# Two projection blocks beside the first layer's attention, and tiles of normalised tokens taken over by output weights chunk by chunk

## The chip, the core and the metric

The kernel runs on one core of a Trainium2 chip, with its engines TensorE (PE; its weight loads are PEld), VectorE (DVE), ScalarE (ACT), GpSimd (POOL) and SyncE (SP), which here only issues DMAs. The metric is the device time of one execution in microseconds. Before the change three timed runs took 2635.68, 2638.16 and 2638.88 us, median 2638.16 us.

## What is computed

One step of a small diffusion backbone with two layers, over 1024 sample tokens and 256 prompt tokens of 1024 features. The change is in layer 0, whose reference is, cut to what matters:

```python
hp = _rmsnorm(yp, norm_g[l]) * (1.0 + sc_p) + sh_p        # normalised tokens, samples alike
qa, ka, va, za, qb, kb, vb, ob, zb, gb = jnp.split(h @ w_in, AB_SPLITS, axis=-1)
attn = _window_attn_latent(_axial_rope(qa, rows, cols), _axial_rope(ka, rows, cols), va, ck, cv, sink)
a_out = attn * jax.nn.silu(za)                            # 16 heads, 4 key/value groups
hb, states = _mlstm_bidir(qb, kb, vb, ob, gb + gate_bias, conv_w, norm_w, init)
b_out = hb * jax.nn.silu(zb)
out = jnp.concatenate([a_out, b_out], axis=-1) @ w_out
yp = yp + gt_p * out_p
```

Layer 1 is a latent attention with its own projections. All products are made in float32r: each operand is split into a high and a low part, and three matmuls (high x high, high x low, low x high) take the place of one.

## The kernel before, in words

The normalised tokens lie transposed in SBUF as `hTh` and `hTl` (high and low), in three chunks of 512, 512 and 256 tokens, each one tile of 8 slices of 128 features. The input projection `h @ w_in` is cut into **blocks** of 256 output columns (`DenseBlock`). A block of attention queries (q) or of its gate (z) has six **units** (`unit_T`), two per chunk; a unit is 24 matmuls into one PSUM bank, of 512 or, for the last chunk, 256 columns. Its cost is 2 or 1, so a block costs 10. `Dense.units` gives the blocks out in pieces, in the order of the list `blocks`, and `Dense.pump` requests and splits the weights of the next block ahead of time.

Layer 0 goes through these stages. First the tokens are normalised and five blocks run with the adaLN rows beside them; here a scheduler of the framework orders the instructions. Then the order is written by hand (`manual_schedule`):

- `beside_memory`: 80 visits of the mLSTM in 174 slots (7 ahead, 2 for each visit, 7 behind), with 24 projection blocks (cost 240) spread evenly over the slots.
- `beside_attention`: the windowed attention of 4 groups x 10 query blocks. `Attention.run` goes through **ticks**. Each tick from 12 to 179 turns one block of 128 keys: PE transposes the probabilities (`turn`), ACT casts them (`split`, L1139) and DVE subtracts (L1140), and a tick later PE multiplies with the values (`weighted`) into one PSUM bank V that ACT and DVE empty at the group's end (`out`). Scores (`scores`), maximum (`peak`, DVE), exponential (`exp`, ACT) and division (`normal`, POOL) run some ticks ahead. `extra(i)` puts other work into tick i: until tick 12 the last block (z3), from tick 25 on **steps** of the output projection, 10 of them up to tick 56 and 150 evenly after that. A step is three matmuls of 512 columns; there are 200 steps over ten matrix rows, of which 160 run beside the attention.
- At tick 17 `release` gives back the token tiles (`hp`), the rope table (`rpool`) and the projection pools, opens the pool `wo1` in their place, and `load_wout` loads ten rows of 512 KB of `w_out`, one every three ticks, and splits each four ticks later in two halves (ACT L824, POOL L825).

The remaining 40 steps, the second half of the output projection and layer 1 follow. A helper issues every matmul (`Kern.mm`, L103), every transpose (L107) and every DMA (L138), so the profile tells these apart by tile names: `mm` is the bank of projections and transposed probabilities, `D` of scores, `V` of weighted values, `att_kh`/`att_q` keys and queries, `w` output weights, `o_ah`/`o_al` the split rows they multiply, `wh`/`wl` input weights.

## Time and profile before

| | |
|---|---|
| median of three timed runs | 2638.16 us |
| the profiled execution's own time | 2633.0 us |
| its span, first to last instruction | 2630.9 us |
| PE, DVE, ACT, POOL busy | 98%, 68%, 54%, 44% of the span |
| DMA | 348.78 MB, mean 133 GB/s |

Busy time is the union of an engine's instructions. Matmuls overlap, so PE can be busy all the time and still have room; the distance between starts tells more. Idle time is given to the engine whose signal ended it.

### The profile page before, as it was taken

The numbers are of one execution on the slowest core, as the hardware profiler recorded it, in microseconds if no ns is written. First come the engines' busy times: TensorE is split into PE (matmuls) and PEld (weight loads), VectorE is DVE, ScalarE is ACT, GpSimd is POOL, SyncE is SP. The second block draws the span as 40 slices with busy tenths as digits, with TensorE's granted clock in tenths as the row PEclk, the third lists the DMA queues.
The fourth block names the chain that finished last, engine by engine and source line by source line (L and its number), as shares of the span: only waits on it lengthen the run. The fifth ranks groups of instructions, "written<-read, shape, count | busy, mean of one in ns | idle before, by whom it ended". The sixth has DMA issues, their size and how long they took to land.

```text
span 2630.9 us, 48195 instructions
## 1 busy us (share of the span) xinstructions
PE 2573.1 (98%) x16209; PEld 2261.5 (86%) x16209; DVE 1782.9 (68%) x4040; ACT 1407.8 (54%) x3598; POOL 1164.6 (44%) x1533
## 2 busy tenths in 40 slices
PE   8999999999999999989999999999999999999998
PEld 6878898898998888878888878987799899999887
DVE  6884565746747566488777554335788888888853
ACT  5232444434533433287666432322788888888842
POOL 5342333423434444275554553223455545555742
PEclk9999999999999999999999999999999999999999
DMA  7465566556656655463433454233310101100333
GB/s 249 153 178 177 160 194 190 175 176 193 205 180 221 199 175 177 144 199 107 133 114 103 154 169 167 84 101 118 95 31 29 48 25 40 36 19 29 123 105 128
DMA packets 344584, 348.78 MB, mean 133 GB/s; under 512 B 29609, under 2 KB 291414, under 8 KB 344082
## 3 DMA queue, kind: packets, MB, share of 16 engines
q1 hardware_dynamic: 344338, 345.71, 42.6%
q8 instruction: 129, 2.11, 0.3%
q14 instruction: 117, 0.96, 0.1%
HBM read 235.09 MB, written 110.51 MB: 131 GB/s over the span
## 4 chain that ended last, share of the span: by engine, by line
PE 82%; DVE 5%; issue 2%; ACT 2%; DMA 2%; POOL 2%; SPq 0%; DVEq 0%; POOLq 0%; ACTq 0%
PE mm L103 34%; PE S L103 28%; PE V L103 8%; PE T L107 6%; PE D L103 3%; PE mm L107 2%; PE T L103 1%; DMA w<-in_w_out_ab 0%; DVE macc L321 0%; DVE att_nm L1114 0%; POOL wl L354 0%; ACT att_p L1119 0%; DMA kh<-scr 0%; DMA mw<-in_w_mod 0%; DVE cmx L2157 0%
## 5 line engine op out<-in xcount | busy, mean ns | idle before, releaser
L354 POOL TENSOR_TENSOR wl<-wf,wh 128x256 fp32r<-128x256 f32 (+2 forms) x288 | 244.4, 875 | 444.0 <-ACT wh L353 416.0
L103 PE MATMUL mm<-hTh,wh 128*128 128x512 f32 (+1 forms) x912 | 328.4, 360 | 0.9 <-DVE scr L620 0.9
L103 PE MATMUL mm<-hTl,wh 128*128 128x512 f32 (+1 forms) x912 | 325.1, 356 | 0.0
L103 PE MATMUL mm<-hTh,wl 128*128 128x512 f32 (+1 forms) x912 | 325.0, 356 | 0.0
L103 PE MATMUL S<-cK,cQ 96*128 96x512 f32 (+3 forms) x1248 | 297.9, 363 | 2.1 <-ACT cPb L2159 1.0
L2207 DVE TENSOR_TENSOR cpl<-T,cph 128x512 fp32r<-128x512 f32 x336 | 228.2, 684 | 37.4 <-ACT cph L2206 33.3
L103 PEld LDWEIGHTS S<-cK,cQ 96*128 96x128 f32 (+1 forms) x1248 | 192.7, 189 | 24.1 <-ACT cPb L2159 2.9
L2206 ACT CAST cph<-T 128x512 fp32r<-128x512 f32 x336 | 192.5, 589 | 26.1 <-PE T L107 13.6
L103 PEld LDWEIGHTS mm<-hTh,wl 128*128 128x128 f32 x912 | 171.7, 188 | 26.6
L103 PEld LDWEIGHTS mm<-hTh,wh 128*128 128x128 f32 x912 | 171.5, 188 | 25.1 <-DVE scr L620 1.1
L103 PEld LDWEIGHTS mm<-hTl,wh 128*128 128x128 f32 x912 | 171.7, 188 | 23.1
L2157 DVE TENSOR_REDUCE cmx<-S 128x1 f32<-128x512 f32 x256 | 172.4, 681 | 15.6 <-PE S L103 14.5
L103 PE MATMUL V<-cph,cV 128*128 128x256 f32 x672 | 176.8, 289 | 0.2 <-DVE cst L2131 0.2
L103 PE MATMUL V<-cpl,cV 128*128 128x256 f32 x672 | 171.9, 284 | 1.3 <-DVE cst L2131 1.3
L2138 POOL TENSOR_SCALAR cPa<-cPa,cst 128x512 f32<-128x512 f32 x128 | 99.7, 779 | 120.6 <-DVE cst L2135 94.3
L103 PE MATMUL S<-w,o_ah 128*128 128x512 f32 x492 | 151.5, 394 | 0.6 <-POOL w L825 0.6
L103 PE MATMUL mm<-w,o_ah 128*128 128x512 f32 x468 | 151.2, 402 | 0.0
L1128 POOL TENSOR_SCALAR att_p<-att_p,att_den 128x640 f32<-128x640 f32 (+1 forms) x128 | 97.7, 777 | 103.3 <-DVE att_den L1125 42.1
L1139 ACT CAST att_ph<-mm 128x512 fp32r<-128x512 f32 x168 | 98.6, 587 | 80.8 <-PE mm L107 78.6
L1140 DVE TENSOR_TENSOR att_pl<-mm,att_ph 128x512 fp32r<-128x512 f32 x168 | 115.7, 689 | 31.7 <-ACT att_ph L1139 26.7
L353 ACT CAST wh<-wf 128x256 fp32r<-128x256 f32 (+2 forms) x288 | 102.2, 410 | 64.3 <-DMA wf<-in_w_in_ab 34.3
L103 PE MATMUL mm<-wh,hTh 128*128 128x256 f32 x480 | 135.6, 283 | 0.0
(432 smaller groups left out, 7832.8 us busy)
## 6 DMA issues: line engine op xcount, KB each, us to landing
wf<-in_w_in_ab SPq DMA_DIRECT2D x120, 256.0 KB
in<-in SPq DMA_DIRECT2D x40, 514.0 KB
in<-in SPq DMA_DIRECT2D x32, 386.0 KB
mw<-in_w_mod SPq DMA_DIRECT2D x48, 256.0 KB
in<-scr SPq DMA_DIRECT2D x40, 258.0 KB
o_x<-y SPq DMA_DIRECT2D x20, 512.0 KB
wm<-in_w_mod SPq DMA_DIRECT2D x16, 512.0 KB
in<-cx SPq DMA_DIRECT2D x32, 256.0 KB
```

Source lines behind the costliest of these rows:

```text
L103: return self.nc.tensor.matmul(out, lhsT, rhs, start=start, stop=stop)
L107: self.nc.tensor.transpose(out, in_, self.ident[:p, :p])
L353: K.nc.scalar.copy(wh, wf[:, k])
L354: K.nc.gpsimd.tensor_sub(wl, wf[:, k], wh.bitcast(F32))
L1128: nc.gpsimd.tensor_scalar(pv, pv, den[:, i:i + 1], 1.0, ALU.mult, ALU.mult)
L1139: K.nc.scalar.copy(ph, self.T)
L1140: K.nc.vector.tensor_sub(pl, self.T, ph.bitcast(F32))
L2138: nc.gpsimd.tensor_scalar(pv, pv, wt[:, c:c + 1], rd, ALU.mult, ALU.mult)
L2157: nc.vector.tensor_reduce(mx[:, b, c:c + 1], S, AX.X, ALU.max, negate=True)
L2206: nc.scalar.copy(ph, T_)
L2207: nc.vector.tensor_sub(pl, T_, ph.bitcast(F32))
```

## The change

The list of blocks becomes q0, z0, q1, z1, q2, q3, z2, z3; before it alternated to the end. 23 blocks run beside the memory stage and two, z2 and z3, beside the attention: z2 until tick 12, z3 from tick 13 to tick 52 in pieces of three matmuls (six of the short chunk), one a tick (`parts = 4`). The output projection's steps begin at tick 61, 160 of them evenly to the attention's end.

The token tiles are cut smaller (`Hidden`): 20 tiles of one shape under one tag `hw`, two (in the last chunk four) slices of features in each. `place_wout` allocates 20 more under the same tag, so each row of output weights takes over the place of tokens whose last reader is z3. It loads halves of 256 KB into four raw buffers `wraw` and splits each three ticks later (six for the last four). The requests stand at ticks 30 to 44, every second, for the place of chunk 0; at 46 to 53, every one, for chunk 1; at 56 to 59 for chunk 2. `release` moves to tick 55 and no longer gives back the tokens' pool.

```diff
@@ -335,6 +335,7 @@
     def __init__(self, K, wp, cols, fn, bufs, width, src="w_in_ab"):
         self.K, self.wp, self.cols, self.fn, self.bufs, self.width = K, wp, cols, fn, bufs, width
         self.src, self.w, self.wf, self.when, self.asked = K.I[src][0], [], [], [], 0
+        self.parts = 2
 
     def ask(self):
         K, F, a = self.K, sum(n for _, n in self.cols), 2 * self.asked
@@ -371,10 +372,24 @@
                     yield u.cost / 2
             units = units[2:]
         for u in units:
-            n = u.cost if self.K.pairs else 2 * u.cost
+            n = u.cost * (1 if self.K.pairs else self.parts)
             for i in range(n):
                 u.products(i, n)
                 yield u.cost / n
+
+
+class Hidden:
+
+
+    def __init__(self, K, pool, N, tiles=None, cols=slice(None)):
+        self.shape, self.cols, self.m = [128, KD, N], cols, D // N
+        self.tiles = tiles or [K.t(pool, [128, self.m, N], F32R, "hw", 20) for _ in range(KD // self.m)]
+
+    def __getitem__(self, key):
+        _, k, s = key
+        if isinstance(k, slice):
+            return Hidden(None, None, self.shape[2], self.tiles, s)
+        return self.tiles[k // self.m][:, k % self.m, self.cols if s == slice(None) else s]
 
 
 class Unit:
@@ -662,11 +677,9 @@
     d["sd"] = [dram([NT, 128, 256], F32R, f"sd{h}") for h in range(4)]
     d["g"] = dram([4, NT, 2, 3, 128], F32, "grow")
 
-    K.hTh, K.hTl = [], []
     hp = right("hT0")
-    for ci, (t0, N) in enumerate(CHUNKS):
-        K.hTh.append(hp.tile([128, KD, N], F32R, tag=f"hh{ci}", name=f"hTh{ci}"))
-        K.hTl.append(hp.tile([128, KD, N], F32R, tag=f"hl{ci}", name=f"hTl{ci}"))
+    hidden = [[Hidden(K, hp, N) for _ in range(2)] for _, N in CHUNKS]
+    K.hTh, K.hTl = [[h[i] for h in hidden] for i in range(2)]
     wp = K.wp = right("w0")
     sp = left("start")
     setup_cond(K, sp)
@@ -730,8 +743,9 @@
     for h in range(4):
         blocks += b_proj(K, wp, tp, h)
     blocks.append(DenseBlock(K, wp, [(O_KA, 256)], partial(a_keys, K), 6, 272))
-    for g in range(4):
-        blocks += a_proj(K, wp, g)
+    qs, zs = zip(*[a_proj(K, wp, g) for g in range(4)])
+    blocks += [qs[0], zs[0], qs[1], zs[1], qs[2], qs[3], zs[2], zs[3]]
+    zs[3].parts = 4
     mp = left("mod")
     dense.mods = mod_steps(K, mp, mods[0:2], 4)
     K.tp = gtp = left("gtmp")
@@ -753,34 +767,43 @@
     K.y1 = [K.t(K.dram, [128, D], F32, f"y1_{t}") for t in range(NT)]
     K.y2 = [K.t(K.dram, [128, D], F32, f"y2_{t}") for t in range(NT)]
     w = I["w_out_ab"][0]
-    opened = []
+    opened = [hp]
+
+    wt = []
 
     def release():
-        for pool in (K.rpool, tp, wp, hp):
+        for pool in (stage, tp, wp):
             pool.release()
         K.ring = None
         p = right("wo1")
         opened.append(p)
-        wt = load_wout(K, p, w, [8, 9, 10, 11, 12, 13, 14, 15, 0, 1])
-        gate = gate_rows(K, p, 0)
+        gate = {}
+
+        def late():
+            gate[0], gate[1] = gate_rows(K, p, 0)
+
+        K.later(late, 8)
         steps = out_steps(K, p, Attention.ORDER, wt, lambda tt: gate[0 if tt < 8 else 1], lambda tt: x_src(K, tt),
                           lambda tt: ((d["bT"][tt], 0, 5), (d["bT"][tt], 5, 8, d["aT"][tt], 0, 2)), lambda tt: K.y1[tt])
         next(steps)
-        return steps
+        return steps, place_wout(K, hp, w, wt, p, [0, 1], 6)
 
     K.set_psum(S=3, mm=3, T=2)
     bp = left("mls")
     K.flow = Flow()
     with K.tc.manual_schedule():
         K.pairs = True
-        beside_memory(K, bp, dense, 24, 240)
+        beside_memory(K, bp, dense, 23, 230)
         K.pairs, K.spread = False, True
         bp.release()
         gp.release()
         K.set_psum(D=2, mm=3, V=1)
         ap = left("att")
         a_sinks(K, ap)
-        steps = beside_attention(K, ap, dense, release)
+        K.rpool.release()
+        stage = right("raw")
+        steps = beside_attention(K, ap, dense, place_wout(K, hp, w, wt, stage, [8, 9, 10, 11, 12, 13, 14, 15], 3),
+                                 release)
     K.flow = None
     ap.release()
     K.set_psum(S=5, T=3)
@@ -788,7 +811,8 @@
     wt = load_wout(K, p, w, range(2, 8))
     for _ in steps:
         pass
-    opened.pop().release()
+    while opened:
+        opened.pop().release()
     hp = K.hp1 = right("hT1")
     K.hTh, K.hTl = [], []
     for ci, (t0, N) in enumerate(CHUNKS):
@@ -811,6 +835,25 @@
             xst = []
     sp.release()
     p.release()
+
+
+def place_wout(K, p, src, wt, stage, ks, lag):
+
+
+    def split(w, wf):
+        wh, wl = w
+        K.nc.scalar.copy(wh, wf)
+        K.nc.gpsimd.tensor_sub(wl, wf, wh.bitcast(F32))
+
+    for k in ks:
+        w = [K.t(p, [128, D], F32R, "hw", 20) for _ in range(2)]
+        wt.append(w)
+        for half in range(2):
+            sl = slice(half * 512, half * 512 + 512)
+            wf = K.t(stage, [128, 512], F32, "wraw", 4)
+            K.dma(wf, src[k * 128:(k + 1) * 128, sl])
+            K.later(partial(split, [t[:, sl] for t in w], wf), lag)
+            yield
 
 
 def load_wout(K, p, src, ks):
@@ -1164,21 +1207,24 @@
         K.later(gated)
 
 
-def beside_attention(K, ap, dense, release):
+def beside_attention(K, ap, dense, place, release):
 
 
     A = Attention(K, ap)
-    units, spent, steps, left = dense.units(1), 0, None, 160
+    units, spent, steps, left = dense.units(2), 0, None, 160
     lead = A.LEAD + 1
-    n = lead + 4
+    n = lead + 42
+    asks = [*range(lead + 17, lead + 33, 2), *range(lead + 33, lead + 41), *range(lead + 43, lead + 47)]
 
     def extra(i):
-        nonlocal spent, steps, left
-        while spent < 10 and spent < max(3, (i + 1) * 10 / lead):
-            spent += next(units, 10)
+        nonlocal spent, steps, left, place
+        while spent < 20 and spent < max(3, (i + 1) * 10 / lead if i < lead else 10 + (i + 1 - lead) / 4):
+            spent += next(units, 20)
         if i == n:
-            steps = release()
-        while i > n + 8 and left > (160 - (i - n - 8) / 3 if i < n + 39 else 150 * (A.end - i) / (A.end - n - 39)):
+            steps, place = release()
+        if i in asks:
+            next(place)
+        while i > n + 5 and left > 160 * (A.end - i) / (A.end - n - 5):
             next(steps)
             left -= 1
 
@@ -1229,11 +1275,11 @@
         if n:
             K.later(lambda: (load_res(i + 1), K.dma(dst(t["tt"]), t["y"])))
 
-    load_res(0)
     load(0, 0)
-    K.later(partial(split, 0, 0), 5)
-    K.later(partial(load, 0, 1), 12)
-    K.later(partial(split, 0, 1), 17)
+    load(0, 1)
+    K.later(partial(split, 0, 0), 3)
+    K.later(partial(split, 0, 1), 5)
+    K.later(partial(load_res, 0), 7)
     yield
     for i in range(len(T)):
         ps = [None, None]
```

Three places in the order of instructions. On PE, at a tick near 13 (`small` is the identity of the transposes), before the change:

```order
L107 MATMUL mm_14361<-small,att_p_14100 128x128 x2
L107 MATMUL mm_14361<-small,att_p_14145 128x128 x2
L103 MATMUL V_14318<-att_ph_14344,att_v 128x512
L103 MATMUL V_14318<-att_pl_14345,att_v 128x512
L103 MATMUL D_14373<-att_kh,att_q_14189 128x384
L103 MATMUL D_14373<-att_kl,att_q_14189 128x384
L103 LDWEIGHTS mbf
L103 MATMUL D_14373<-mbf 128x128
L103 LDWEIGHTS mbf
L103 MATMUL D_14373<-mbf 128x128
L103 MATMUL D_14373<-att_kh,att_q_14189 128x256
L103 MATMUL D_14373<-att_kl,att_q_14189 128x256
```

and now, where `hw` are token tiles and `wh`, `wl` the weights of z3:

```order
L107 MATMUL mm_14132<-small,att_p_13928 128x128 x2
L107 MATMUL mm_14132<-small,att_p_13973 128x128 x2
L103 MATMUL mm_14162<-hw_129,wh_13870 128x512
L103 MATMUL mm_14162<-hw_133,wh_13870 128x512
L103 MATMUL mm_14162<-hw_129,wl_13871 128x512
L103 MATMUL V_14166<-att_ph_14103,att_v 128x512
L103 MATMUL V_14166<-att_pl_14104,att_v 128x512
L103 MATMUL D_14169<-att_kh,att_q_14017 128x384
L103 MATMUL D_14169<-att_kl,att_q_14017 128x384
L103 LDWEIGHTS mbf
L103 MATMUL D_14169<-mbf 128x128
L103 LDWEIGHTS mbf
```

Between the transposes and the next product with the values stand three matmuls of z3, one piece; before, that place held nothing in most of these ticks.

On POOL, around ticks 49 to 56 now (`L846` is the subtraction for the output weights, before at L825):

```order
L846 TENSOR_TENSOR hw_15259<-wraw_15260,hw_15258 128x512
L1204 TENSOR_TENSOR att_o_15323<-att_o_15323,att_z_15148 128x256
L1171 TENSOR_SCALAR att_p_15307<-att_p_15307,att_den_15309 128x512 x2
L846 TENSOR_TENSOR hw_15259<-wraw_15294,hw_15258 128x512
L846 TENSOR_TENSOR hw_15339<-wraw_15340,hw_15338 128x512
L1171 TENSOR_SCALAR att_p_15387<-att_p_15387,att_den_15389 128x640 x2
L846 TENSOR_TENSOR hw_15339<-wraw_15369,hw_15338 128x512
L846 TENSOR_TENSOR hw_15414<-wraw_15415,hw_15413 128x512
L1204 TENSOR_TENSOR att_o_15473<-att_o_15473,att_z_15302 128x256
L1171 TENSOR_SCALAR att_p_15457<-att_p_15457,att_den_15459 128x640 x2
L846 TENSOR_TENSOR hw_15414<-wraw_15443,hw_15413 128x512
L1171 TENSOR_SCALAR att_p_15533<-att_p_15533,att_den_15535 128x640 x2
```

and before, around ticks 37 to 43, where the same subtractions stood:

```order
L1128 TENSOR_SCALAR att_p_14893<-att_p_14893,att_den_14895 128x640 x2
L1220 TENSOR_TENSOR o_al_14938<-o_a_14784,o_ah_14937 128x384
L825 TENSOR_TENSOR w_14942<-w_14438,w_14941 128x512
L1128 TENSOR_SCALAR att_pp_14958<-att_pp_14958,att_den_14960 128x256 x2
L825 TENSOR_TENSOR w_15028<-w_14439,w_15027 128x512 x2
L1128 TENSOR_SCALAR att_pp_15010<-att_pp_15010,att_den_15012 128x256 x2
L1161 TENSOR_TENSOR att_o_15051<-att_o_15051,att_z_14923 128x256
L825 TENSOR_TENSOR w_15120<-w_14440,w_15119 128x512
L1128 TENSOR_SCALAR att_p_15077<-att_p_15077,att_den_15079 128x640 x2
L825 TENSOR_TENSOR w_15120<-w_14440,w_15119 128x512
L1128 TENSOR_SCALAR att_p_15136<-att_p_15136,att_den_15138 128x640 x2
L825 TENSOR_TENSOR w_15200<-w_14441,w_15199 128x512
```

The subtractions have moved to later ticks and stand as closely between the divisions `att_p`, one tick's worth each.

On ACT, near the end of the start stage, the casts of tokens into their high part, before (`hTh_129`, `131`, `133` are the three chunks):

```order
L537 CAST hTh_133<-xT_169 128x256 x3
L262 ACTIVATE mrow_433<-S_416 2x256
L537 CAST hTh_133<-xT_169 128x256
L537 CAST hTh_129<-xT_167 128x512
L537 CAST hTh_131<-xT_168 128x512
L537 CAST hTh_133<-xT_169 128x256
L262 ACTIVATE mrow_485<-S_468 2x256
L537 CAST hTh_129<-xT_167 128x512
L537 CAST hTh_131<-xT_168 128x512
L537 CAST hTh_133<-xT_169 128x256
```

and now (`hw_129` to `132` are chunk 0, `137` to `140` chunk 1, `145` and `146` chunk 2):

```order
L552 CAST hw_131<-xT_181 128x512
L262 ACTIVATE mrow_595<-S_578 2x256
L552 CAST hw_132<-xT_181 128x512
L552 CAST hw_137<-xT_182 128x512 x2
L552 CAST hw_138<-xT_182 128x512 x2
L552 CAST hw_132<-xT_181 128x512
L552 CAST hw_139<-xT_182 128x512 x2
L552 CAST hw_140<-xT_182 128x512 x2
L552 CAST hw_145<-xT_183 128x256 x4
L552 CAST hw_146<-xT_183 128x256 x4
```

Chunks 1 and 2 were cast as their slices came; now they all stand behind the last tile of chunk 0.

## Rows read from the trace of the kernel before

**Rows 1.** The page: PE's busy time, and the granted clock in 40 slices, in tenths.

```profile
PE 2573.1 (98%) x16209; PEld 2261.5 (86%) x16209; DVE 1782.9 (68%) x4040; ACT 1407.8 (54%) x3598; POOL 1164.6 (44%) x1533
...
PEclk9999999999999999999999999999999999999999
```

**Rows 2.** The table of stretches: from and to in us from the span's start, the length, then busy us (instructions) of PE, PEld, DVE, ACT and POOL, granted clock, DMA share and GB/s.

```profile
260.00:1084.00 824.00, 821.76 (x5338) 744.05 (x5337) 501.92 (x1281) 341.64 (x914) 319.83 (x391) 1.00 0.60 184
1084.00:1109.00 25.00, 25.00 (x147) 21.35 (x146) 8.44 (x21) 6.46 (x15) 3.37 (x5) 1.00 0.55 169
1109.00:1191.00 82.00, 74.04 (x470) 59.01 (x469) 68.58 (x156) 69.59 (x161) 61.00 (x72) 1.00 0.63 187
1191.00:1209.00 18.00, 16.90 (x108) 13.76 (x107) 14.80 (x32) 12.57 (x28) 8.49 (x11) 1.00 0.27 76
1209.00:1484.00 275.00, 275.00 (x1678) 233.45 (x1677) 211.44 (x460) 185.22 (x422) 140.79 (x182) 1.00 0.38 112
1484.00:1600.00 116.00, 114.74 (x521) 93.37 (x520) 50.42 (x78) 36.06 (x69) 59.24 (x52) 1.00 0.60 195
```

**Rows 3.** The timeline of PE at the end of the memory stage and in the lead: start, duration, and the matmul; between the first two rows stand 30 like them, between the last two 11.

```profile
1083.81 0.39 PE L103 MATMUL mm<-hTl,wh 128*128 128x512 f32 x1
...
1091.00 0.39 PE L103 MATMUL mm<-hTh,wl 128*128 128x512 f32 x1
1091.23 0.28 PE L103 MATMUL D<-att_kh,att_q 128*128 128x256 f32 x1
...
1102.74 0.28 PE L103 MATMUL mm<-hTh,wh 128*128 128x256 f32 x1
...
1104.16 0.34 PE L103 MATMUL D<-att_kh,att_q 128*128 128x384 f32 x1
```

**Rows 4.** The cast that each tick makes once, in the stretches 1109 to 1191, 1191 to 1209 and 1209 to 1484 us: count, duration in ns, first and last start. The first stretch ends with the cast that opens the next.

```profile
L1139 ACT CAST att_ph<-mm x41: 576/587/607, 1109.1 to 1190.6; 128x512 fp32r<-128x512 f32 x41
...
L1139 ACT CAST att_ph<-mm x8: 573/586/588, 1190.6 to 1206.9; 128x512 fp32r<-128x512 f32 x8
...
L1139 ACT CAST att_ph<-mm x120: 584/587/597, 1209.0 to 1483.5; 128x512 fp32r<-128x512 f32 x120
```

**Rows 5.** Groups of PE by shape: the matmuls of the output projection from 1109 to 1191 us (first two) and from 1209 to 1484 us: count, busy us, mean ns.

```profile
L103 PE MATMUL mm<-w,o_ah 128*128 128x512 f32 x18 | 5.8, 404 | 0.0
L103 PE MATMUL mm<-w,o_al 128*128 128x512 f32 x9 | 3.6, 395 | 0.0
...
L103 PE MATMUL mm<-w,o_ah 128*128 128x512 f32 x289 | 92.8, 402 | 0.0
L103 PE MATMUL mm<-w,o_al 128*128 128x512 f32 x144 | 57.0, 396 | 0.0
```

**Rows 6.** The view of waits of PE (1085 to 1195 us) and of ACT (1109 to 1195 us), the longest of each: us in total, times, longest.

```profile
PE V L103 <- DVE att_o L1158: 5.2, 8, 1.3
...
ACT att_p L1119 <- DVE att_nm L1114: 5.9, 10, 0.9
ACT att_ph L1139 <- PE mm L107: 4.2, 8, 1.1
ACT att_p L1119 <- POOL att_pp L1128: 1.0, 1, 1.0
```

**Rows 7.** The view of waits of PE in the memory stage, 260 to 1110 us, its longest.

```profile
PE mm L103 <- DVE scr L620: 0.9, 1, 0.9
```

**Rows 8.** Durations: the gate's multiplication and tanh of a z unit (min/median/max ns, 1084 to 1120 us); then POOL's groups from 1109 to 1191 us and ACT's cast of output weights; then, from the timelines of SP and ACT, the issue of a weight load and the cast that reads it.

```profile
L645 DVE SCALAR_TENSOR_TENSOR scr<-scr,mm x6: 422/686/689, 1083.7 to 1113.6; 128x512 f32<-128x512 f32 x4, 128x256 f32<-128x256 f32 x2
...
L644 ACT ACTIVATE scr<-mm x5: 373/586/599, 1088.6 to 1113.2; 128x512 f32<-128x512 f32 x3, 128x256 f32<-128x256 f32 x2
...
L825 POOL TENSOR_TENSOR w<-w,w 128x512 fp32r<-128x512 f32 x20 | 25.7, 1288 | 4.5 <-ACT w L824 3.0 <-DVE D L1113 0.7 <-POOL att_p L1128 0.7
L1128 POOL TENSOR_SCALAR att_p<-att_p,att_den 128x640 f32<-128x640 f32 x24 | 19.0, 804 | 12.6 <-DVE D L1113 7.9 <-DVE att_den L1125 4.7
L1161 POOL TENSOR_TENSOR att_o<-att_o,att_z 128x256 f32<-128x256 f32 x9 | 6.7, 742 | 0.7 <-DVE att_o L1158 0.7
L1128 POOL TENSOR_SCALAR att_p<-att_p,att_den 128x512 f32<-128x512 f32 x7 | 4.8, 695 | 1.2 <-DVE D L1113 1.2
L1128 POOL TENSOR_SCALAR att_pp<-att_pp,att_den 128x256 f32<-128x256 f32 x8 | 3.7, 483 | 3.8 <-DVE D L1113 3.8
...
L824 ACT CAST w<-w 128x512 fp32r<-128x512 f32 x20 | 12.3, 615 | 0.0
...
1167.12 1.39 SPq L138 DMA_DIRECT2D w<-in_w_out_ab  x1
...
1173.00 0.62 ACT L824 CAST w<-w 128x512 fp32r<-128x512 f32 x1
```

**Rows 9.** The start of the program: a stretch of the table, columns as in rows 2; the casts of tokens (min/median/max ns, 0 to 260 us); and the first block's matmuls from 50 to 62 us.

```profile
50.00:60.00 10.00, 7.10 (x51) 5.75 (x49) 9.50 (x24) 5.45 (x14) 5.38 (x5) 0.83 0.19 55
...
L537 ACT CAST hTh<-xT x24: 400/615/627, 25.6 to 63.1; 128x512 fp32r<-128x512 f32 x16, 128x256 fp32r<-128x256 f32 x8
...
L103 PE MATMUL S<-wh,hTh x7: 432/432/596, 57.6 to 61.8; 128*128 128x272 f32 x7
```

**Rows 10.** The view of waits of SP, 1085 to 1230 us: us in total, times, longest.

```profile
SPq L138 <- POOL att_o L1161: 24.2, 9, 5.1
SPq L138 <- PE mm L107: 18.7, 9, 6.1
...
SPq L138 <- POOL o_al L1220: 10.5, 3, 7.3
```

**Rows 11.** Two stretches of the table at the start of layer 1, columns as in rows 2.

```profile
1830.00:1840.00 10.00, 8.12 (x43) 6.60 (x41) 8.52 (x19) 3.24 (x7) 6.45 (x5) 0.83 0.39 146
1840.00:1850.00 10.00, 5.60 (x25) 4.39 (x25) 7.88 (x13) 3.79 (x8) 3.02 (x3) 0.93 0.58 209
```

## The prediction

> **What bounds the kernel now.** I read the page's busy shares first [rows 1]: PE is busy 98% of the span at a granted clock of 0.9 or more in every slice, so only PE's own work, or a stretch where PE is not truly full, can move the time. The second view is the table of stretches [rows 2], cut at the places that the change speaks of: the memory stage (the mLSTM with projection blocks beside it, 260 to 1084 us), the attention's lead (1084 to 1109), its first 40 ticks with an output (1109 to 1191; a tick is one pass of the attention's loop), the next 8 ticks (to 1209), the last 120 (to 1484), and the output projection's rest. The reader is to see that PE is busy 821.8 of 824 us in the memory stage and all of 275 us in the last 120 ticks, but only 74.0 of 82 us in the 40 ticks.
>
> Busy time hides how full PE is there, because matmuls overlap. So the third view gives the pitch: 32 matmuls of 512 columns start between 1083.81 and 1091.23 us, 0.232 us each, and 12 of 256 columns between 1102.74 and 1104.16, 0.118 us each [rows 3]. The fourth gives the pace of the ticks by the cast that each tick makes once: 40 ticks from 1109.1 to 1190.6 us (2.04 us a tick), 8 to 1209.0 (2.30), 120 to 1484 (2.29) [rows 4].
>
> In the last 120 ticks the output projection has 289 + 144 = 433 matmuls [rows 5], 433 x 0.232 = 100.5 us, so the attention itself takes (275 - 100.5) / 120 = 1.45 us of PE a tick. In the 40 ticks there are 18 + 9 = 27 such matmuls [rows 5], 6.3 us: PE needs 40 x 1.45 + 6.3 = 64.4 us of the 81.5. About 17 us of PE are free there. What holds the pace is the chain from engine to engine: PE waits for the values' bank that DVE empties (5.2 us in 8 waits), ACT for DVE's maxima (5.9 us) and for PE's transposes (4.2 us) [rows 6], with DVE busy 68.6, ACT 69.6 and POOL 61.0 of the 82 us [rows 2]. In the memory stage the longest PE wait that the view of waits gives is 0.9 us [rows 7]; nothing is free.
>
> **The change part by part.** *One block leaves the memory stage.* A block is four units of 24 matmuls with 512 columns and two of 24 with 256: 96 x 0.232 + 48 x 0.118 = 22.3 + 5.7 = 28.0 us. PE is full there, the number of slots stays 174, and the other engines have room (DVE 502, ACT 342 of 824 us [rows 2]), so I take all of it: **-28.0 us**. By the bounds: no less than nothing, if some chain of the visits set the pace instead, which the one wait of 0.9 us excludes.
>
> The Trainium skill, "TensorE: Matmul & The Clock Gate", section "Wait — 56ns, not 53.3ns?", gives 215.7 ns between warm matmuls of 512 columns, start to start. The trace has 0.232 us [rows 3], and the measurement decides; by the page's formula of columns over 2.4 GHz plus 2.5 ns the block would be an estimated 96 x 0.216 + 48 x 0.109 = 26.0 us, the steps that come later 10.2 instead of 10.9, and the sum some 1.3 us less gain.
>
> *The lead* keeps ten units of cost, now of z2 instead of z3. What is new is that z3's weights are split here: 8 casts and 8 subtractions, beside an ACT that is busy 6.5 and a POOL that is busy 3.4 of 25 us [rows 2], while PE is full. Nothing; without that cover it would be some 3 us (8 x 0.4).
>
> *z3 in the 40 ticks.* One piece a tick, 28.0 / 40 = 0.70 us of PE. Its other work is six tanh and six multiplications (0.59 and 0.69 us at most [rows 8]), 7 us over 82 on two engines that have 12 to 13 us free each. Two ends for the pace. If PE alone sets it: 1.45 + 0.70 = 2.15 us a tick. If each piece stands serially in the chain that sets the pace now: 2.04 + 0.70 - 0.16 (the 6.3 us of output steps that it replaces, a tick) = 2.58. Between them lies a measured point: the last 120 ticks carry 100.5 / 120 = 0.84 us of side work a tick and go at 2.29, the 40 carry 0.16 and go at 2.04. On that line 0.70 gives 2.04 + 0.54 x 0.25 / 0.68 = 2.24 us. I take it: 40 x 2.24 = 89.6 against 81.5, **+8.1 us**.
>
> *Ticks 52 to 60* have no side work at all now: z3 is done, the output projection begins at tick 60. I take the pace of the poorly filled ticks, 2.04: 16.3 against 18.4 us, **-2.1 us**.
>
> *The output projection* still has 160 steps beside the attention. By tick 60 it has done 160 - 433/3 = 15.7 of them now; these move into the last 120 ticks, where PE is full: 15.7 x 3 x 0.232 = **+10.9 us**.
>
> *The output weights.* Twenty casts of 0.61 us on ACT and twenty subtractions of 1.29 us on POOL stay twenty [rows 8]; they move from ticks 22 to 50 to ticks 33 to 56 and 62 to 65. In ticks 49 to 56 one falls in each tick: POOL then has 1.29 us beside 19.0 + 6.7 + 4.8 + 3.7 = 34.2 us over 40 ticks [rows 8], 0.86, so 2.15 us a tick, just its pace. Scores stand several ticks ahead, so I count nothing, and a microsecond or two for the range. The loads are halves of 256 KB with 3 ticks from request to cast, 6.7 us. A full 512 KB tile that was issued at 1167.12 was cast at 1173.00 [rows 8], 5.9 us, and ACT's longest waits hold no load [rows 6]. Behind such a wait on ACT stand the exponentials and the casts of the transposes, that is the whole chain; this is the slower rival below. The tiles they overwrite are free by then: chunk 0's last unit ends at tick 28, its first cast is at tick 33; chunk 1 at 44 and 49; chunk 2 at 52 and 62.
>
> *Start of the program.* By the order, the casts of chunks 1 and 2 now come after chunk 0's. All 16 exposed would be 8 x 0.615 + 8 x 0.40 = 8.1 us [rows 9] slower; the wait of PE in 50 to 60 us gone (7.1 of 10 busy) would be 2.9 faster. PE begins the first block at 57.6 with chunk 0's tokens [rows 9], and four token tiles of 24 matmuls lie before chunk 1 is read, so I take 0. The second layer's order shifts a few rows too; 0, with some 3 us either way.
>
> **Sum:** -28.0 + 8.1 - 2.1 + 10.9 = -11.1 us. The profiled execution took 2633.0 us (span 2630.9), so 2621.9 on its footing; the median of the timed runs, 2638.2, lies 5.2 us above it, so the forecast is **2627 us**. In general the sum is 40p - 100.7 for a pace p in the 40 ticks.
>
> **The rivals.** *The block is hidden wholly* (p stays 2.04): -19.2, 2619 us. For it: 17 us free. Against: PE's own count is 2.15. *Each piece is serial* (p = 2.58): +2.5, 2641 us, no change. For it: in the order a piece stands ahead of the first product of each group, the very one that waits [rows 6]. Against: the last 120 ticks carry more and go at 2.29. *Raw halves come late, the slower side.* SP issues in order and already stands up to 7.3 us for POOL and up to 6.1 for PE [rows 10]; only four raw buffers exist, so the fifth load waits for POOL's subtraction of the first, and ACT then stands at the cast. It eats the gain at 11.1 / 16 = 0.7 us for each of 16 casts, is slower beyond measurement at 1.0 us, and at 1.5 us gives +13, 2651 us. Against: no such wait today, and the loads are half as large. *The start is exposed*: +8.1, so 2635 us.
>
> One more comes from the clock. At 1830 to 1850 PE was busy 8.12 and then 5.60 of 10 us and its granted clock was 0.83 and 0.93 [rows 11], part of the time at the lower level; in the 40 ticks with 74.0 of 82 us it was 1.00 [rows 2]. If ticks 52 to 60 fell to the lower level, 8 x 1.45 = 11.6 us of PE work would double to 23.2, 6.9 over the 16.3: 2634 us. The Trainium skill's page on TensorE, Part 1, says that idleness throttles the array to half rate; the trace agrees at 1830 us, and this speaks against leaving eight ticks bare.
>
> **How the numbers follow.** Forecast 0.56 (p from 2.15 to 2.40, its own range 2620 to 2634), hidden 0.07, serial 0.16, late halves 0.12, start exposed 0.06, clock 0.03. Within 0.2% (5.3 us, about what a measurement here tells from no change) is 2633 to 2643. Faster: nearly all of the forecast, the hidden case and a little of the serial one, 0.65. Slower: the late halves and a serial pace over 2.65, 0.15. The rest, 0.20, is no change. The range 2616 to 2641 takes in the hidden case with 3 us and reaches to the serial one.
>
> **What would show it.** The memory stage should end some 28 us earlier with PE as full as now; the 40 ticks should take 86 to 96 us with PE near 80 of them and matmuls of z3 in each; the next 8 about 16; the last 120 about 286. The forecast is wrong if the cast of raw halves on ACT waits for DMA, if the pace passes 2.5, or if the memory stage gives back clearly less than 28.

## The result and the profile after

The changed kernel takes 2642.15 us (median of 10 runs, 2637.39 to 2645.69), the kernel before 2635.48 us beside it (10 runs). The ratio is 1.0025, 95% interval 1.0016 to 1.0035: slower by 0.25%. The forecast was 2627 us and faster. The profiled execution took 2642.5 us with a span of 2640.7, 9.8 more than the span of before. All medians here and below are of fast runs; one run of 7210 us, with the casts on DVE, is left out as slow.

The page of the changed kernel, PE's busy time and the granted clock in 40 slices, answers to [rows 1]:

```profile
PE 2573.7 (97%) x16209; PEld 2262.2 (86%) x16209; DVE 1780.5 (67%) x4040; ACT 1409.5 (53%) x3598; POOL 1159.2 (44%) x1533
...
PEclk9989999999999999999999999999999999999999
```

The number of matmuls is the same and so is PE's busy time; the span is not. One digit has fallen, the third slice (132 to 198 us), in the start of the program, where the prediction had put a zero.

The table of stretches, cut at the same events as [rows 2] (first projection matmul of the memory stage, first scores, ticks 12, 52, 60 and 179; columns as there):

```profile
241.10:1077.00 835.90, 830.91 (x5384) 751.57 (x5384) 502.71 (x1296) 347.55 (x923) 317.49 (x394) 1.00 0.62 187
1077.00:1094.90 17.90, 17.90 (x117) 15.55 (x116) 7.99 (x20) 7.07 (x17) 4.91 (x7) 1.00 0.72 224
1094.90:1185.50 90.60, 89.37 (x577) 76.35 (x577) 71.84 (x161) 68.27 (x156) 47.15 (x60) 1.00 0.41 126
1185.50:1204.10 18.60, 15.31 (x101) 12.09 (x100) 14.82 (x33) 16.08 (x37) 16.42 (x18) 1.00 0.79 239
1204.10:1490.20 286.10, 285.30 (x1717) 240.72 (x1717) 212.97 (x461) 186.67 (x429) 149.21 (x190) 1.00 0.39 115
```

The same cuts are laid in the trace of before by the starts of the same instructions. Every number is a difference of two starts, in us:

| stretch | before | after | difference | predicted |
|---|---|---|---|---|
| start, to the first projection matmul of the memory stage | 230.1 | 241.1 | +11.0 | 0 |
| memory stage, to the first scores | 861.1 | 835.9 | -25.2 | -28.0 |
| lead, to tick 12 | 17.9 | 17.9 | 0 | 0 |
| 40 ticks, 12 to 52 | 81.5 | 90.6 | +9.1 | +8.1 |
| ticks 52 to 60 | 18.4 | 18.6 | +0.2 | -2.1 |
| ticks 60 to 179 | 274.5 | 286.1 | +11.6 | +10.9 |
| rest, to the end | 1147.4 | 1150.5 | +3.1 | 0 |
| sum | 2630.9 | 2640.7 | +9.8 | -11.1 |

The ticks are read from the cast that each makes once, the counterpart of [rows 4]:

```profile
L1182 ACT CAST att_ph<-mm x40: 577/587/593, 1094.9 to 1182.8; 128x512 fp32r<-128x512 f32 x40
...
L1182 ACT CAST att_ph<-mm x8: 580/587/589, 1185.5 to 1202.0; 128x512 fp32r<-128x512 f32 x8
...
L1182 ACT CAST att_ph<-mm x120: 581/587/590, 1204.1 to 1490.2; 128x512 fp32r<-128x512 f32 x120
```

So the attention paid back about what was expected. The surprise is at the start. There the view of waits of PE (50 to 260 us: total, times, longest) reads, for the changed kernel:

```profile
PE T L107 <- DVE LI L1409: 6.0, 1, 6.0
PE S L103 <- DVE macc L321: 5.1, 1, 5.1
PE T L107 <- DVE GI L1338: 2.9, 1, 2.9
```

and for the kernel before:

```profile
PE S L107 <- ACT mrow L262: 2.9, 2, 2.7
PE S L103 <- DVE bmod L306: 2.4, 1, 2.4
PE T L107 <- ACT rst L1372: 2.2, 1, 2.2
PE T L107 <- DVE LI L1363: 1.6, 1, 1.6
```

`GI` and `LI` are gate rows of the mLSTM, `macc` sums of modulation rows; all three come from DVE. The waits for `mrow` lie ahead of the first block. The other three of before, with two of 0.3 us that follow them in the view, make 6.8 us and compare with 14.0 us of after: 7.2 more. From the first block's first matmul to the memory stage's first one it is 172.5 us in before (57.6 to 230.1) and 182.8 in after (58.3 to 241.1). The remaining 3.1 of these 10.3 us fit the clock. Over these two stretches the rows of PE (length, busy, instructions, granted clock, DMA share, GB/s), after and then before, are

```profile
58.30:241.10 182.80, 168.84 (x1086) 0.94 0.50 151
57.60:230.10 172.50, 165.66 (x1087) 0.97 0.53 160
```

An estimate from them: 0.06 x 182.8 less 0.03 x 172.5 is 5.8 us more of the full clock lost, and the part of it that fell into the waits cost nothing more; how much that was is not measured. Shorter windows of the changed kernel, then the same places in before:

```profile
100.00:110.00 10.00, 7.13 (x41) 0.83 0.55 176
140.00:150.00 10.00, 4.03 (x27) 0.67 0.25 62
150.00:160.00 10.00, 10.00 (x54) 0.82 0.36 90
180.00:190.00 10.00, 8.13 (x32) 0.66 0.82 246
```

```profile
100.00:110.00 10.00, 10.00 (x62) 1.00 0.24 73
140.00:150.00 10.00, 7.76 (x54) 0.83 0.33 93
150.00:160.00 10.00, 10.00 (x48) 1.00 0.80 237
180.00:190.00 10.00, 8.71 (x73) 1.00 0.80 243
```

The three waits begin at 102.7 (`GI`), 140.9 (`LI`) and 176.8 us (`macc`); each fall of the clock lies at one of them or right behind it. By these rows the array ran part of the time at 1.2 GHz there, and a microsecond of waiting then cost more than itself. The Trainium skill ("TensorE: Matmul & The Clock Gate", Part 1) says that activity releases the throttle and idleness brings it back; these rows agree.

Whose lateness is it? The subtractions that split the normalised tokens, on DVE, in the changed kernel and in before (min/median/max ns, first and last start):

```profile
L553 DVE TENSOR_TENSOR hw<-xT,hw x12: 412/826/1785, 28.7 to 72.4; 128x512 fp32r<-128x512 f32 x8, 128x256 fp32r<-128x256 f32 x4
```

```profile
L538 DVE TENSOR_TENSOR hTl<-xT,hTh x12: 407/686/1605, 26.3 to 63.2; 128x512 fp32r<-128x512 f32 x8, 128x256 fp32r<-128x256 f32 x4
```

The last one starts 9 us later, and behind it on DVE stand the modulation's first sum (67.0 us before, 73.7 after) and the gates: `GI` is written at 105.2 us against 100.8, and `LI`, for which PE waits longest, 12 us later than before. Its row in the changed kernel, then in before:

```profile
L1409 DVE TENSOR_TENSOR LI<-LI,gB x1: 1475/1475/1475, 145.2 to 145.2; 36x1280 f32<-36x1280 f32 x1
```

```profile
L1363 DVE TENSOR_TENSOR LI<-LI,gB x1: 2020/2020/2020, 133.2 to 133.2; 36x1280 f32<-36x1280 f32 x1
```

The change put all twenty token tiles under one tag, and in the order of the built program their first writes now stand as the program is written, chunk after chunk; before, each chunk had tags of its own and the casts of chunks 1 and 2 stood among those of chunk 0.

### The profile page after: what moved, and what is told of

It reads as the page before. It is cut to its first block, busy times and chain, and to the rows that moved or that the text cites. A ratio compares the mean times of both kernels' runs of the same rounds, so it can differ in the third digit from the quotient of the medians.

```text
span 2640.7 us, 48207 instructions
## 1 busy us (share of the span) xinstructions
PE 2573.7 (97%) x16209; PEld 2262.2 (86%) x16209; DVE 1780.5 (67%) x4040; ACT 1409.5 (53%) x3598; POOL 1159.2 (44%) x1533
## 4 chain that ended last, share of the span: by engine, by line
PE 81%; DVE 4%; DMA 3%; issue 3%; POOL 2%; ACT 2%; SPq 0%; POOLq 0%; DVEq 0%; ACTq 0%
PE mm L103 34%; PE S L103 25%; PE V L103 9%; PE T L107 6%; PE D L103 4%; PE mm L107 3%; PE T L103 1%; DMA o_x<-y 1%; POOL wl L355 1%; DMA mw<-in_w_mod 0%; DVE macc L321 0%; POOL w L917 0%; DMA wk<-in_w_kvb_c 0%; SPq L138 0%; DMA w<-in_w_out_ab 0%
## 5 line engine op out<-in xcount | busy, mean ns | idle before, releaser
L103 PE MATMUL mm<-hw,wh 128*128 128x512 f32 (+1 forms) x1824 | 494.0, 359 | 0.9 <-DVE scr L635 0.9
L103 PEld LDWEIGHTS mm<-hw,wh 128*128 128x128 f32 x1824 | 315.8, 188 | 48.1 <-DVE scr L635 1.1
L103 PE MATMUL mm<-hw,wl 128*128 128x512 f32 (+1 forms) x912 | 325.1, 356 | 0.0
L103 PEld LDWEIGHTS mm<-hw,wl 128*128 128x128 f32 x912 | 171.7, 188 | 26.7
L103 PE MATMUL mm<-wh,hw 128*128 128x256 f32 x960 | 177.3, 282 | 4.0 <-DVE scr L1496 3.9
L103 PEld LDWEIGHTS mm<-wh,hw 128*128 128x128 f32 x960 | 149.7, 188 | 4.6 <-DVE scr L1496 4.6
L103 PE MATMUL mm<-wl,hw 128*128 128x256 f32 x480 | 134.8, 281 | 0.1
L103 PE MATMUL S<-w,o_ah 128*128 128x512 f32 x432 | 133.3, 395 | 1.1 <-POOL w L868 0.8
L103 PEld LDWEIGHTS V<-cph,cV 128*128 128x128 f32 x672 | 126.5, 188 | 8.0 <-issue 1.7
L103 PEld LDWEIGHTS V<-cpl,cV 128*128 128x128 f32 x672 | 126.7, 189 | 7.1 <-DVE cst L2177 1.7
```

Source lines behind the costliest of these rows:

```text
L103: return self.nc.tensor.matmul(out, lhsT, rhs, start=start, stop=stop)
```

## The experiments

Ratios are to the kernel before, run beside it on the same chip, with their 95% intervals. Each trace is of one execution.

**A tag for each place.** In the changed kernel, each of the twenty places has a tag of its own (`K.place` numbers them in turn); which output weights follow which tokens stays the same.

```
-        self.tiles = tiles or [K.t(pool, [128, self.m, N], F32R, "hw", 20) ...
+        self.tiles = tiles or [K.t(pool, [128, self.m, N], F32R, K.place("hw"), 1) ...
...
-        w = [K.t(p, [128, D], F32R, "hw", 20) for _ in range(2)]
+        w = [K.t(p, [128, D], F32R, K.place("hw"), 1) for _ in range(2)]
```

> The changed kernel with a tag of its own for each of the 20 places that tokens and output weights share; nothing else differs. Theory T (the shared tag makes the scheduler write the token tiles in the order of their allocation, so DVE's subtractions for chunks 1 and 2 fall behind 58 us, into the part of the start where DVE is full): the first projection matmul of the memory stage comes at 230 to 234 us as before the change, not at 241, and the ratio to the kernel before is 0.996 to 1.000. Rival U (the late start comes from something else in the change or from chance): first such matmul at 238 us or later, ratio 1.002 or more.

Measured: 2634.61 us, ratio 0.9989 (0.998 to 0.9998). The first projection matmul stands at 233.0 us, 172.1 after the first block's first. The subtractions are done earlier:

```profile
L557 DVE TENSOR_TENSOR hw<-xT,hw x12: 406/688/1604, 28.6 to 66.6; 128x512 fp32r<-128x512 f32 x8, 128x256 fp32r<-128x256 f32 x4
```

T holds by the place and by the ratio: of the changed kernel's time, (1.0025 - 0.9989) x 2636.7 = 9.5 us are the shared tag at the start, and without it the change is a gain, if a small one. The trace is of the longest of this kernel's runs (2639.06 us). In it the clock fell in ticks 52 to 60 too, to a mean of 0.91, where the table above has 1.00 for the changed kernel. The row of PE:

```profile
1180.60:1199.70 19.10, 16.23 (x102) 0.91 0.78 223
```

This bears on every later experiment that takes this kernel as its base.

**The shared tag alone.** The kernel before, with only its token tiles cut in twenty and put under one tag.

```
-        K.hTh.append(hp.tile([128, KD, N], F32R, tag=f"hh{ci}", name=f"hTh{ci}"))
-        K.hTl.append(hp.tile([128, KD, N], F32R, tag=f"hl{ci}", name=f"hTl{ci}"))
+    hidden = [[Hidden(K, hp, N) for _ in range(2)] for _, N in CHUNKS]
```

> The kernel before with the smaller token tiles under one tag and nothing else of the change. Theory T: the start alone costs its full price, the first projection matmul of the memory stage at 239 to 243 us, ratio 1.003 to 1.0045. Rival U: 230 to 233 us, ratio 1.000.

Measured: 2643.68 us, ratio 1.0027 (1.0017 to 1.0038). The first projection matmul stands at 240.7 us; from the first block's first matmul it is 182.8 us, the changed kernel's own number. Waits of PE from 50 to 260 us, and two windows:

```profile
PE T L107 <- DVE LI L1375: 6.0, 1, 6.0
PE S L103 <- DVE macc L321: 4.6, 1, 4.6
PE T L107 <- DVE GI L1304: 2.6, 1, 2.6
```

```profile
140.00:150.00 10.00, 4.05 (x25) 0.66 0.26 63
180.00:190.00 10.00, 8.54 (x35) 0.66 0.82 246
```

The same three waits and the same clock, with nothing moved beside the attention; the ratio is a little smaller than T named, the place is T's. Together with the first experiment, which cuts the tiles just as finely under separate tags, this shows the tag at work and not the tiles' size.

**The same tag, another order.** The changed kernel, with the token tiles loaded earlier: in the string, `x` starts a token tile and `m` one of the eight feature slices of the modulation that the tokens take.

```
-    for n, a in enumerate("mxmxmxmxmxmxmxmxxx"):
+    for n, a in enumerate("mxxmxxmxxmxxmxxmmm"):
```

> The changed kernel with its shared tag kept, but with the token tiles loaded earlier among the conditioning's blocks (order mxxmxxmxxmxxmxxmmm in place of mxmxmxmxmxmxmxmxxx), so that in the written program the casts and subtractions of chunks 1 and 2 stand before the last ones of chunk 0. Theory T: with one tag the first writes keep the order in which the program is written, and with the old loading order that puts 16 casts and their subtractions behind chunk 0's last one, on a DVE that then starts the modulation rows late. Written in the other order, the shared tag costs nothing: the first projection matmul of the memory stage falls from 241 us to 230 to 236, and the ratio from 1.0025 to 0.997 to 1.000. Theory U: the shared tag costs by itself, whatever the order: the first such matmul stays at 238 or later and the ratio at 1.002 or more.

Measured: 2635.81 us, ratio 0.9997 (0.9988 to 1.0005). The first projection matmul stands at 232.5 us, 172.0 after the first block's first, and of the waits of PE from 50 to 260 us the longest are

```profile
PE T L107 <- DVE scr L1466: 2.3, 1, 2.3
PE T L107 <- DVE GI L1338: 1.8, 1, 1.8
PE S L103 <- POOL wl L355: 1.4, 2, 1.2
```

The first line is the wait for `LI`: the matmul that waits is the transposition of `LI`, and the clearing of `scr` that the profile names ended at the same moment as `LI`. T's place and ratio hold: with the same tag and another written order the cost is gone. The edit also moves the modulation's slices among the token tiles, so it does not change the first writes alone. One thing does not fit a simple shift of lateness: here the last subtraction starts at 69.6 us, only 2.8 earlier than in the changed kernel, `LI` at 142.5, only 2.7 earlier, and `GI` is no earlier (106.3 against 105.2 us), yet the waits of 6.0 and 5.1 us have shrunk to 2.3 and 0.5. Which link of DVE's order makes those two waits stays open.

**One block fewer.** The kernel before without block z2; its output differs.

```
-        blocks += a_proj(K, wp, g)
+        blocks += a_proj(K, wp, g)[:1 if g == 2 else 2]
+    d["sza"][2] = d["sza"][1]
...
-        beside_memory(K, bp, dense, 24, 240)
+        beside_memory(K, bp, dense, 23, 230)
```

> The kernel before without the block z2: group 2 of the attention takes the gate of group 1 in its place, 23 blocks run beside the memory stage, z3 beside the attention as before. Theory M (PE is full in the memory stage): it is 28 us shorter, 25.5 to 30, ratio 0.988 to 0.991, with start and attention unchanged. Rival N (the visits have a pace of their own, and a block takes less than its matmuls with it): 20 to 24 us shorter, ratio above 0.9915.

Measured: 2613.47 us, ratio 0.9913 (0.9899 to 0.9926). The memory stage takes 836.1 us (232.7 to 1068.8), 25.0 less than before's: between M and N. The missing three answer to new waits in the view of waits of PE, here (first fence) and in the changed kernel, where the longest of before was 0.9 us [rows 7]:

```profile
PE mm L103 <- DVE scr L1451: 4.5, 3, 2.9
PE mm L103 <- DVE scr L620: 0.9, 1, 0.9
```

```profile
PE mm L103 <- DVE scr L1496: 3.9, 2, 2.9
PE mm L103 <- DVE scr L635: 0.9, 1, 0.9
```

L1451 and L1496 are the same statement in the two kernels, the subtraction that empties the bank of a unit of values (`v_split`).

**Another block behind the convolution.** The first experiment's kernel, with the blocks of values and of the output gate exchanged.

```
-            ... (O_VB, by_token(v_split)), (O_OB, by_token(o_tanh)), (O_ZB, z_block))]
+            ... (O_OB, by_token(o_tanh)), (O_VB, by_token(v_split)), (O_ZB, z_block))]
```

> The kernel of the first experiment (a tag for each place), with the values' block of each mLSTM head placed behind the output gate's block instead of in front of it. Theory V: three to four of the 28 us that the memory stage was to give up are lost where the values' first units stand right behind the keys' convolution: DVE is busy with the taps and the banks of products are not emptied (3.9 us in two waits). With the output gate's block between them, emptied by ACT alone, the waits on the values' subtraction fall under 1 us, the stretch from the first projection matmul to the first attention score falls from 837 to 832 to 835 us, and the ratio from 0.9989 to 0.9965 to 0.9985. Theory P: the waits are only where the stage's slack shows, another wait takes their place: 836 us or more and a ratio of 0.998 to 1.001.

Measured: 2632.93 us, ratio 0.999 (0.9981 to 0.9999). The stage takes 834.4 us (228.2 to 1062.6), inside V's range, but the ratio is P's. The changed kernel and the four versions of it that keep the old order of these blocks and show no fall of the clock in this stage take 835.7 to 835.9, so the exchange is worth about 1.4 us; the first experiment's 837.1 holds such a fall (0.83 from 710 to 720 us). The wait has shrunk a little and changed its name:

```profile
PE mm L107 <- ACT scr L1506: 3.0, 2, 2.4
PE mm L107 <- DVE scr L639: 0.9, 1, 0.9
```

L1506 is the output gate's tanh. V's remedy gives little: in both orders tried, the block behind the convolution has its banks emptied late. Why the stage has these waits with one block fewer and not with all was not settled.

**z3 in 32 ticks.** The first experiment's kernel, with z3 at a faster pace and the rest following sooner.

```
-    n = lead + 42
-    asks = [*range(lead + 17, lead + 33, 2), *range(lead + 33, lead + 41), *range(lead + 43, lead + 47)]
+    n = lead + 34
+    asks = [*range(lead + 14, lead + 22), *range(lead + 26, lead + 34), *range(lead + 35, lead + 39)]
...
-        ... 10 + (i + 1 - lead) / 4):
+        ... 10 + (i + 1 - lead) * 10 / 32):
```

> The kernel of e1 with z3 in 32 instead of 40 ticks, and requests of weights, release and output steps eight ticks earlier. Theory P (what the 40 ticks and the bare ticks lose is PE's free time, and a denser piece a tick does not stretch the chain beyond PE's need): ticks 12 to 179 take 3 to 6 us less than the 395 of the changed kernel, ratio to the kernel before 0.994 to 0.998. Rival Q (the chain sets the pace, denser pieces wait in it): no shorter than 394, ratio equal to e1 or above.

Measured: 2637.78 us, ratio 0.9997 (0.9989 to 1.0006). Ticks 12 to 179 take 396.8 us, the first experiment's 396.6 over again. P fails by its numbers and Q's hold. Part of what the denser pieces gain is lost in new waits of PE, here from 1085 to 1206 us:

```profile
PE D L107 <- DMA att_q<-ql: 3.4, 1, 3.4
PE V L107 <- DVE att_o L1205: 2.2, 2, 1.1
```

The first is a wait for queries that a DMA brings, and it lies in the ticks without side work, here 44 to 52, where the clock fell as well:

```profile
1163.80:1186.10 22.30, 15.74 (x96) 0.94 0.78 222
```

They take 22.3 us against the 18.6 of the changed kernel's ticks 52 to 60, so Q's reason, a chain that denser pieces wait in, is not shown by this run.

**Half of the output weights.** The first experiment's kernel, with rows 12 to 15 not loaded or split.

```
+        if k in (12, 13, 14, 15):
+            K.placed += 2
+            wt.append(wt[k - 12])
+            yield
+            yield
+            continue
```

> The kernel of the first experiment (a tag for each place), without the second eight tiles of output weights: rows 12 to 15 of the output weights are not loaded or split, and the tiles of rows 8 to 11 are read in their place, so the output differs. What it leaves out is the eight casts on ACT and eight subtractions on POOL in ticks 48 to 56. Theory W: these casts and subtractions slow the ticks in which they stand, because PE's products with the values wait behind a cast on ACT; without them ticks 48 to 60 take 25.5 to 27 us instead of 29.8 (28.4 in the changed kernel), and the ratio is 0.9965 to 0.9985. Theory B: ticks without side work have a pace of their own of 2.3 us, whatever ACT and POOL do beside; then ticks 48 to 60 take 28 us or more and the ratio stays at 0.998 to 1.000.

In the changed kernel and in the first experiment, the longest wait of PE in the ticks around 48 to 60 is for a cast of output weights on ACT; without those casts the longest is another. The three in that order (1080 to 1215, 1165 to 1205, 1160 to 1200 us):

```profile
PE V L103 <- ACT hw L845: 2.0, 1, 2.0
```

```profile
PE V L107 <- ACT hw L849: 2.0, 1, 2.0
```

```profile
PE V L107 <- DVE D L1166: 1.6, 1, 1.6
```

Measured: 2629.94 us, ratio 0.9973 (0.9963 to 0.9982). Ticks 48 to 60 take 26.3 us, as W said: 2.1 less than in the changed kernel, at a clock of 1.00 in ticks 52 to 60 of both. (Of the 3.4 us against the first experiment a part is the fall of the clock there.) But ticks 12 to 179 take 394.9, against 395.3 in the changed kernel and 394.9 in the version with another loading order: by tick 179 the gain is given back. So the casts do slow the ticks in which they stand, but the lower ratio is not explained by them. The mean granted clock over the timed runs is higher here, 0.995 against 0.9935 in the first experiment, which goes the same way; that this is the cause is not shown.

**The casts on DVE, and an earlier output projection.** Two kernels, measured together. The second has both edits:

```
+        if k >= 12:
+            K.nc.vector.tensor_copy(wh, wf)
+        else:
+            K.nc.scalar.copy(wh, wf)
```

```
-        while i > n + 5 and left > 160 * (A.end - i) / (A.end - n - 5):
+        while i > n + 3 and left > 160 * (A.end - i) / (A.end - n - 3):
```

> The kernel of the first experiment (a tag for each place), with the casts of the output weights' rows 12 to 15, which stand in ticks 48 to 56, moved from ACT to DVE. Theory W, refined: what those ticks lose is ACT's time, since each cast stands ahead of an exponential or a cast of transposes that PE's products wait for; DVE is not in that place at that moment. Ticks 48 to 60 then take 26.5 to 28.5 us instead of 29.8, PE's wait for a cast of weights is gone, and the ratio is 0.9970 to 0.9988. Theory S: DVE is in the same chain (it empties the scores and the values' bank), so the cast costs as much there, and POOL's subtractions go on: 29 us or more, ratio 0.9985 to 1.000.

> The same kernel as the other of this call, with the output projection's steps beginning two ticks earlier, at tick 58, and spread over the attention from there. Theory F: ticks 52 to 60 leave PE room (8 ticks of 1.45 us of the attention's matmuls, 11.6 us, in the 18 to 19 that they take), and the six steps or so that fall in them cost less there than in the last 120 ticks, where PE is full: ticks 12 to 179 take 1.0 to 2.5 us less than in the other kernel of this call, and the ratio is 0.0003 to 0.0010 lower. Theory G: the chain from engine to engine, not PE, sets those ticks, and each step lengthens them by about what it saves later: a difference of under 0.7 us either way, ratios within 0.0003.

Measured: 2634.12 us, ratio 0.9989 (0.9979 to 0.9998) with the casts on DVE; 2635.5 us, ratio 0.9996 (0.9987 to 1.0004) with both. Ticks 48 to 60 take 29.6 us with the first edit: the same wait, longer, now for ACT's cast of transposes (1165 to 1200 us):

```profile
PE V L107 <- ACT att_ph L1189: 2.2, 1, 2.2
PE V L107 <- DVE att_o L1208: 1.2, 1, 1.2
```

Ticks 12 to 179 take 396.8 and 396.3 us. S holds against the first experiment, whose trace has the same fall of the clock in these ticks (0.91 there, 0.92 here). Of G the difference in the ticks holds (0.5 us); the ratios lie 0.0007 apart, more than G said and not the way of F, but their intervals overlap.

Ticks 12 to 179 in all kernels: 374.4, 374.4 and 374.6 us without z3 in them (before, the shared tag alone, one block fewer); 394.9 to 396.9 us in all eight with it. Of these eight, the three whose clock stayed at 1.00 in the ticks without side work take 394.9 to 395.3, and the five in which it fell there (0.91 to 0.94) take 396.3 to 396.9.

## Why the prediction was wrong

- **The start, predicted 0, measured +11.0 us: the step that failed.** The prediction saw in the order that the casts of chunks 1 and 2 now come behind chunk 0's, priced all of them exposed at 8.1 us, and took 0 because PE has four token tiles to do before it reads chunk 1. That looked at the wrong reader and the wrong engine. PE is not held up by chunk 1's tokens; it is held up 44 to 118 us after the first block's first matmul by gates and modulation rows that DVE makes behind its subtractions, 14.0 us in three waits. The rival "the start is exposed" had 0.06; its 8.1 us was a sum of ACT's casts, so that it comes near the measured 11.0 is in part luck: the wait on DVE's rows and the lower clock that went with it are not in it.
- **The memory stage, predicted -28.0, measured -25.2.** The mechanism is right, the size is 10% off. The step "the one wait of 0.9 us excludes" other limits read a wait that was absent in before as one that could not come. With a block fewer it came: 3.9 us in the changed kernel, 4.5 in the kernel with one block fewer.
- **The 40 ticks, predicted +8.1, measured +9.1.** The pace is 2.265 us against 2.24; the line between the two measured paces was a good guide, and both ends, 2.15 and 2.58, would have been worse. PE is now busy 89.4 of 90.6 us, where the forecast said near 80.
- **Ticks 52 to 60, predicted -2.1, measured +0.2.** The pace of poorly filled ticks was taken (2.04); it was 2.33. The prediction had left the casts and subtractions of weights at nothing, "a microsecond or two for the range"; in ticks 48 to 60 they are worth 2.1 us (28.4 against 26.3), of which 1.2 fall in ticks 52 to 60. Without them these ticks still take 17.4 us, 1.1 more than forecast. The rival of raw halves that come late was not the reason: ACT waited 0.6 us for them (1175 to 1205 us), one time. The clock stayed at 1.00 in these ticks here, but the rival of the clock, given 0.03, was a near thing: in five of the versions above it fell in them, to 0.91 to 0.94, though not for the whole of them.
- **The last ticks, predicted +10.9, measured +11.6.** From 1204.1 to 1491 us there are 477 matmuls of the output projection where [rows 5] counts 433, and 44 x 0.232 = 10.2 us:

```profile
L103 PE MATMUL mm<-hw,o_ah 128*128 128x512 f32 x318 | 101.7, 401 | 0.0
L103 PE MATMUL mm<-hw,o_al 128*128 128x512 f32 x159 | 62.9, 396 | 0.0
```

- **The rest, predicted 0, measured +3.1.** From tick 179 to the end, the eleven kernels profiled take 1147.4 to 1151.5 us with nearly the same work, and the two experiments that keep before's attention take 1148.5 and 1149.5. The eight with the change average 1149.9 and the three without it 1148.5. I count this as scatter from run to run; one trace of each does not show whether the 1.4 us are a cost of the change.

With the start mended by a tag for each place, the change is worth -2.9 us (ratio 0.9989), not -11.1. The difference of 8.2 us has no single cause. In the changed kernel's trace 2.8 us of it lie in the memory stage and 4.0 in the attention (+20.9 from tick 12 to 179, where +16.9 were forecast); in the first experiment's own, with a fall of the clock in both, they are 4.0 and 5.3. The attention hides 5.5 to 7.5 of a block's 28 us, in the two paces of z3 that were tried. The best of the versions that do all the work reach 0.9989 to 0.999, which is a gain of less than the 0.2% that the prediction called measurable.

## What to carry to other kernels

When buffers are shared to save space, ask what order their first writes must now take, and follow the engine that makes those writes to everything queued behind it: the reader that waits may be another one, far later. A stretch in which PE shows no wait is full only for the work it holds now; take a block out and a wait that was hidden can appear. Work moved beside a stage with slack should be priced at what a pace between two measured paces gives, not at the slack, and even that can be low: here it gave 16.9 us for the attention, and 28 us of work cost 20.5 to 22.5 in the arrangements tried. Before a small difference between two traces is put down to an edit, compare the granted clock of the same stretch in both.

## What was not expected of the hardware

In the start, waits of 2.9, 6.0 and 5.1 us each went with a fall of the mean granted clock, to 0.83, 0.67 and 0.66 over the 10 us around them, so that part of PE's work ran at 1.2 GHz. In ticks 52 to 60 of the changed kernel PE was idle 3.3 of 18.6 us, with a longest wait of 2.0 us, and the clock stayed at 1.00; in the first experiment's trace the same ticks, with the same longest wait of 2.0 us and PE idle 2.9 of 19.1, had a mean clock of 0.91. So waits alike in length went once with a fall and once without. A wait in a stretch that was full before it can cost more than its own length, and the view of waits alone does not show it: the windows with the granted clock must be read beside it.
